# Tokens kept by residue modulo 4 in each tile of 128, and mixer D's bias table laid out whole

## The chip, the cores and the metric

The kernel runs on one core of a Trainium2 chip. The metric is the device time of one execution in microseconds (us); smaller is better.

## What is computed

Two layers of an encoder trunk over 512 tokens of 1024 features, all in float32. Each layer is a norm, one combined projection to the queries, keys and values of four attention mixers (A, B, C, D) and to four gate blocks, the mixers, their gated sum, an output projection, and an MLP:

```
h = rms_norm(x, attn_norm_g)
q, k, v of A, B, C, D and four gates = split(h @ w_in)
a = mixer_window_gqa(...)       # |i-j| <= 128
b = mixer_dilated(...)          # head groups: |i-j| <= 64 with step 1, <= 256 with step 4, <= 1024 with step 16
c = mixer_differential(...)     # dense, two softmaxes subtracted
d = mixer_neighbourhood(...)    # tokens as 8 rows x 64 columns, 16 columns seen, learned relative bias
x = x + (sum of sigmoid(gate) * (branch @ w_branch)) @ w_out
x = x + relu(rms_norm(x, mlp_norm_g) @ w_up)^2 @ w_down
```

In the second and third head group of B a query sees only tokens of its own residue modulo 4 (modulo 16).

## The kernel before

The 512 tokens are four tiles of 128. The normed input lies transposed in SBUF as two tiles `h_hi` and `h_lo` [128 features, 8, 512 tokens]: each float32 number is kept as a short-mantissa part (fp32r) and the rest of it. A product of two such operands is three matmuls on TensorE (PE), `mm3`, lines 285 to 287: hi by hi, hi by lo, lo by hi. With tokens on the output's partitions (`tm_steps`) the stationary operand is a block of `h`, 128 features by 128 tokens, and the weights stream past it; with features on the partitions (`fm_steps`) the weights are stationary. Each matmul has a weight load of its own ("PEld" in the profile), which may run beside the matmul before it.

Weights come as [128, 768] or [128, 512] units (`unit`): a DMA on the SyncE queue (SP) into `w_raw`, a rounding on ScalarE (ACT) into `w_hi`, a subtraction on VectorE (DVE) into `w_lo`. The first five units' subtraction runs on GpSimd (POOL), line 252.

`project` makes the queries, keys and values of a pair of heads for the token tiles t = 0 to 3. Lines 517 and 524 are those that the first part of the change is about:

```
toks = slice(t, S, NT) if order == "perm" else slice(t * P, (t + 1) * P)
...
if plain:
    nc.scalar.copy(vt[:, t, 0:4:3, :], pv)
```

Mixer B has `order == "perm"`: its token tile t is made of the tokens t, t+4, t+8 and so on, so the stationary block is taken from `h` with a step of four elements of 4 bytes. B has three such chunks in a layer, each with 4 token tiles, 8 feature tiles and 3 matmuls: 288 in a layer, 576 in all. All other blocks of `h` are taken with step one. `qk_norm` and `halves` then norm, rotate and split the heads, and `turn_heads` transposes them on PE and writes them to a `stack` tile [128, 2, 512] with `evacuate` on ACT (line 563). In the order "col" of mixer D that write puts token r * 64 + c at column c * 8 + r, so it has a step of 8 elements (32 bytes). B's order is "perm" and is written straight, 512 elements at a time. `turn_values` (line 572) reorders D's values in the same way, and `store` writes the outputs of B and D back to the tokens' order with a step in what it writes.

`plain` chunks are the second and third head group of B. Their values are copied from PSUM by one ACT instruction for a token tile.

Mixer D's mask tile `d_full` is the mask less the relative bias. The bias comes by 16 DMAs for each head (lines 774 to 776), each to 8 partitions; 128 in all, issued on SP, which also issues the weights' DMAs in its program order.

The order in which the chunks are projected is the list `STREAM`. A planner (`Plan`) interleaves these projections with the heads' attention by an estimate of what it has given to each engine, and the tile framework then sorts the instructions of each engine once more by a simulated time line. So a change of an instruction's shape can move others.

Of the kernel before, what the change touches and what calls it, by code (L numbers as in the profile page):

```python
# [10 lines left out]
F32 = mybir.dt.float32  # L11
# [8 lines left out]
P = 128  # L20
# [48 lines left out]
# Slots of the attention's tiles.  # L69
# [11 lines left out]
class Job:  # L81
    """A column chunk of the projections; left counts what is still to be put in place."""
# [80 lines left out]
class Net:  # L163
# [16 lines left out]
    def setup(self):  # L180
# [6 lines left out]
        self.rope64p = c.tile([P, 2, NT, 32], F32, name="rope64p")  # L187
        self.rope32n = c.tile([P, 2, NT, 16], F32, name="rope32n")
        nc.sync.dma_start(self.rope64n, I["rope64n"])
        nc.sync.dma_start(self.rope64p, I["rope64p"])  # L190
# [34 lines left out]
    def rsqrt(self, pool, ss, n, scale, tag, eng=None):  # L225
        """1 / sqrt(ss * scale + EPS) for a [128, n] tile."""
# [15 lines left out]
    def unit(self, layer, name, k0, kk, segs):  # L242
# [6 lines left out]
        if len(self.W.units) <= NPOOL:  # L249
            # The other engines are still at the first norm.  # L250
# [31 lines left out]
    def mm3(self, ps, st, mv, first, last):  # L282
        """ps += st.T @ mv for split operands (hi, lo); what both parts lack lies below float32."""
# [6 lines left out]
    def tm_steps(self, ps, act, toks, units):  # L290
        """Tokens on partitions: ps[128 tokens, n] = act[:, toks].T @ W."""
# [5 lines left out]
    def fm_steps(self, ps, act, units, c0, toks=slice(0, S)):  # L297
        """Features on partitions: ps[128 features, tokens] = W[:, c0:c0+128].T @ act."""
# [15 lines left out]
    def squares(self, pool, x, ms):  # L314
        """The sum of x^2 / D over the columns at hand."""
# [8 lines left out]
    def norm(self, pool, X, ms, g):  # L324
        """ms: for each token tile the parts of the mean square."""
# [77 lines left out]
    def flat_gain(self, pool):  # L403
        """The gains of mixer d, the queries' part times minus the scale."""
# [7 lines left out]
    def qk_norm(self, pool, ps, t, nq, nk, dh, rope=None, flat=None):  # L412
        """Norm and rotation of the nq + nk heads in ps[128 tokens, heads * dh]; [128, heads, dh]."""
# [61 lines left out]
    def project(self, pool, layer, job, order, segs, nq, nk, dh, rope=None, flat=None, plain=False, vcols=True):  # L475
        """One column chunk [q heads | k heads | v of a pair] for all tokens, transposed. job.q has
# [314 lines left out]
    def mixer_b(self, pool, layer):  # L791
        memo = {}

        def rope():
            if "r" not in memo:
                memo["r"] = self.rope_tables(pool, "b", self.rope64p)
# [422 lines left out]
```

## Time and profile before

| | |
|---|---|
| three executions | 1920.71, 1917.41, 1920.71 us (median 1920.71) |
| span of the profiled execution, first to last instruction | 1919.2 us |
| the profiled execution's own time | not told apart from the three; its span is 1.5 us below their median |
| busy: PE, weight loads, DVE, ACT, POOL | 1858.9, 1674.0, 1138.0, 852.6, 370.9 us |
| mean granted clock of TensorE | 0.990 of full speed |

Two attention stages, about 35 to 560 us and 985 to 1510 us, alternate with two MLPs. In the attention stages mixer D comes first, then A, B and C. [...] PE's busy time overlaps for neighbouring matmuls, so it is read best by the distance of their starts.

### The profile page before, as it was taken

The page shows a single profiled execution, that of the slowest core. Times are in us where ns is not written, and L with a number is a line of the kernel's source. Part 1 is how long each engine was busy: PE and PEld are TensorE (multiplying, and loading weights), DVE is VectorE, ACT ScalarE, POOL GpSimd, SP SyncE. Part 2 cuts the span into 40 slices and gives each one's busy share as a digit, 9 for nine tenths or more (in the row PEclk, how much of TensorE's full clock was granted, in tenths as well). Part 3 has the DMA queues.
Part 4 walks back from the last instruction along what each step waited for, and adds up shares of the span by engine and source line. Part 5 has one row for each costly group of instructions (what it writes and reads, how often), then busy time and mean ns, then how long its engine had stood idle before and what let it go on. Part 6 is the DMA issues. An engine that isn't in the chain of part 4 may idle for free.

```text
span 1919.2 us, 28303 instructions
## 1 busy us (share of the span) xinstructions
PE 1858.9 (97%) x10112; PEld 1674.0 (87%) x10112; DVE 1138.0 (59%) x2571; ACT 852.6 (44%) x1775; POOL 370.9 (19%) x1167
## 2 busy tenths in 40 slices
PE   6998999998999999999999899999999999999999
PEld 5997998886889899989989789988878898989899
DVE  6688756686665543443476876666876564443433
ACT  4666554555443432232357654545554344232321
POOL 3352353441200000000024604433512000000000
PEclk9999999998999999999999999999999999999999
DMA  4322122121242332333343211222222422233323
GB/s 155 102 81 75 50 70 76 50 79 57 77 147 87 105 96 88 88 96 98 122 131 90 86 50 42 76 70 61 68 64 81 146 86 93 88 102 99 94 88 107
DMA packets 70909, 168.96 MB, mean 88 GB/s; under 512 B 9456, under 2 KB 14704, under 8 KB 70768
## 3 DMA queue, kind: packets, MB, share of 16 engines
q1 hardware_dynamic: 70768, 167.16, 28.6%
q8 instruction: 79, 1.29, 0.3%
q14 instruction: 62, 0.51, 0.1%
HBM read 162.93 MB, written 4.19 MB: 87 GB/s over the span
## 4 chain that ended last, share of the span: by engine, by line
PE 82%; DVE 6%; POOL 4%; ACT 3%; issue 3%; DMA 2%; SPq 0%; POOLq 0%; DVEq 0%; ACTq 0%
PE mm L285 25%; PE mm L286 24%; PE mm L287 24%; PE tp L222 3%; PE s L594 2%; PE y L621 1%; POOL rs_w_qk L236 1%; PE y L620 1%; POOL rs_w_qk L235 1%; ACT stack L563 1%; DVE w_lo L216 1%; POOL rs_y_qk L238 1%; POOL rs_w_qk L237 1%; DMA w_raw<-in_wflat 1%; DMA x<-in_x 1%
## 5 line engine op out<-in xcount | busy, mean ns | idle before, releaser
L215 ACT CAST w_hi<-w_raw 128x768 fp32r<-128x768 f32 (+1 forms) x409 | 313.0, 772 | 430.9 <-PE mm L287 241.0
L216 DVE TENSOR_TENSOR w_lo<-w_raw,w_hi 128x768 fp32r<-128x768 f32 (+1 forms) x409 | 362.7, 892 | 191.0 <-ACT w_hi L215 164.9
L285 PE MATMUL mm<-h_hi,w_hi 128*128 128x512 f32 (+1 forms) x1104 | 425.9, 388 | 0.9 <-ACT h_hi L215 0.7
L286 PE MATMUL mm<-h_lo,w_hi 128*128 128x512 f32 (+1 forms) x1104 | 422.5, 384 | 1.4 <-DVE h_lo L216 1.4
L287 PE MATMUL mm<-h_hi,w_lo 128*128 128x512 f32 (+1 forms) x1104 | 416.8, 385 | 1.2 <-POOL w_lo L252 1.2
L287 PEld LDWEIGHTS mm<-h_hi,w_lo 128*128 128x128 f32 x1104 | 209.2, 190 | 41.5 <-POOL w_lo L252 1.7
L285 PEld LDWEIGHTS mm<-h_hi,w_hi 128*128 128x128 f32 x1104 | 209.0, 190 | 40.8 <-ACT h_hi L215 1.2
L286 PEld LDWEIGHTS mm<-h_lo,w_hi 128*128 128x128 f32 x1104 | 209.7, 190 | 39.5 <-DVE h_lo L216 1.8
L287 PE MATMUL mm<-w_hi,u_lo 128*128 128x384 f32 (+1 forms) x768 | 241.9, 319 | 0.0
L286 PE MATMUL mm<-w_lo,u_hi 128*128 128x384 f32 (+1 forms) x768 | 241.2, 319 | 0.0
L285 PE MATMUL mm<-w_hi,u_hi 128*128 128x384 f32 (+1 forms) x768 | 236.4, 319 | 0.0
L235 POOL TENSOR_TENSOR rs_w_qk<-rs_y_qk 128x4 f32<-128x4 f32 (+2 forms) x216 | 56.3, 261 | 782.5 <-DMA d_bias<-in_rel 455.9
L285 PE MATMUL mm<-w_hi,h_hi 128*128 128x384 f32 (+1 forms) x576 | 201.3, 355 | 3.3 <-ACT w_hi L215 1.4
L286 PE MATMUL mm<-w_lo,h_hi 128*128 128x384 f32 (+1 forms) x576 | 201.8, 352 | 0.3 <-DVE w_lo L216 0.2
L287 PE MATMUL mm<-w_hi,h_lo 128*128 128x384 f32 (+1 forms) x576 | 200.7, 350 | 0.0
L1081 DVE TENSOR_TENSOR x<-x,mm 128x384 f32<-128x384 f32 (+1 forms) x120 | 60.9, 508 | 186.9 <-PE mm L287 179.3
L287 PEld LDWEIGHTS mm<-w_hi,u_lo 128*128 128x128 f32 x768 | 143.7, 188 | 0.0
L285 PEld LDWEIGHTS mm<-w_hi,u_hi 128*128 128x128 f32 x768 | 143.1, 188 | 0.5
L286 PEld LDWEIGHTS mm<-w_lo,u_hi 128*128 128x128 f32 x768 | 143.2, 188 | 0.0
L285 PEld LDWEIGHTS mm<-w_hi,h_hi 128*128 128x128 f32 x576 | 135.4, 237 | 5.6 <-ACT w_hi L215 1.6
L286 PEld LDWEIGHTS mm<-w_lo,h_hi 128*128 128x128 f32 x576 | 136.4, 237 | 2.2 <-DVE w_lo L216 0.8
L287 PEld LDWEIGHTS mm<-w_hi,h_lo 128*128 128x128 f32 x576 | 136.4, 237 | 0.7
(166 smaller groups left out, 2916.7 us busy)
## 6 DMA issues: line engine op xcount, KB each, us to landing
w_raw<-in_wflat SPq DMA_DIRECT2D x296, 384.0 KB
w_raw<-in_wflat SPq DMA_DIRECT2D x112, 256.0 KB
x<-in_x SPq DMA_DIRECT2D x8, 512.0 KB
d_full<-in_mask_d SPq DMA_DIRECT2D x8, 448.0 KB
d_bias<-in_rel SPq DMA_DIRECT2D x128, 12.0 KB
x_save<-x SPq DMA_DIRECT2D x4, 512.0 KB
x<-x_save SPq DMA_DIRECT2D x4, 512.0 KB
out_y<-x SPq DMA_DIRECT2D x8, 192.0 KB
```

What stands on the lines that cost most here:

```text
L215: self.nc.scalar.copy(hi, src)
L216: self.nc.vector.tensor_tensor(lo, src, hi.bitcast(F32), op=ALU.subtract)
L222: self.nc.tensor.transpose(out, in_, self.ident_r if short else self.ident)
L235: eng.tensor_tensor(w, y, y, op=ALU.mult)
L236: eng.tensor_tensor(w, w, v, op=ALU.mult)
L237: eng.tensor_scalar(w, w, -0.5, 1.5, op0=ALU.mult, op1=ALU.add)
L238: eng.tensor_tensor(y, y, w, op=ALU.mult)
L285: nc.tensor.matmul(ps, st[0], mv[0], start=first, stop=False)
L286: nc.tensor.matmul(ps, st[0], mv[1], start=False, stop=False)
L287: nc.tensor.matmul(ps, st[1], mv[0], start=False, stop=last)
L594: self.nc.tensor.matmul(ps, q[:, qc], k[:, kc], start=i == 0, stop=i == len(ks) - 1)
L1081: nc.vector.tensor_tensor(x, x, ps[:, 0:w], op=ALU.add)
```

## The change

The tokens are put in another order on the host before the kernel and back after it. Within each tile of 128, place 32 * a + m holds token 4 * m + a: all tokens of one residue modulo 4 lie together. Then:

- B's projections take token tiles of step one, as the others do. The sorting into residue classes moves to `turn_heads`: two writes of 256 elements in runs of 32, in place of one write of 512. B's rotary table `rope64p` and its DMA go.
- The values of a plain chunk are put into their residue class by four ACT copies of 32 partitions, in place of one of 128.
- The first head group's scores read the keys in runs of 32 elements, and the mask in four blocks.
- D's reordering (stacks, values, the store) has runs of 4 elements (16 bytes) where it had single elements. A block of 128 places still holds 16 columns of all 8 rows. B's store has runs of 32.
- D's bias table is laid out on the host for all 128 query places, and comes by one DMA for each head: 8 in all in place of 128.
- The masks are made for the new order. Their sizes stay.

```
-            toks = slice(t, S, NT) if order == "perm" else slice(t * P, (t + 1) * P)
+            toks = slice(t * P, (t + 1) * P)
...
                 if plain:
-                    nc.scalar.copy(vt[:, t, 0:4:3, :], pv)
+                    for c in range(NT):
+                        nc.scalar.copy(vt[32 * t:32 * t + 32, c, 0:4:3, :], pv[32 * c:32 * c + 32])
...
             if order == "col":
-                r0 = (t // 2) * 4
+                g0 = (t // 2) * 16
                 for j in range(2):
-                    dst = st[:, j, :].rearrange("p (c r) -> p r c", r=8)[:, r0:r0 + 4, :]
-                    self.evacuate(dst, src[:, j].rearrange("p u (r c) -> p (u r) c", c=64))
+                    dst = st[:, j, :].rearrange("p (b g e) -> p g b e", b=4, e=4)[:, g0:g0 + 16]
+                    self.evacuate(dst, src[:, j].rearrange("p u (g b e) -> p (u g) b e", b=4, e=4))
+            elif order == "perm":
+                a0 = t - 1
+                for j in range(2):
+                    dst = st[:, j, :].rearrange("p (c a m) -> p a c m", c=NT, m=32)[:, a0:a0 + 2]
+                    self.evacuate(dst, src[:, j].rearrange("p u (c m) -> p u c m", m=32))
...
-        self.nc.scalar.copy(v_t.rearrange("p (c r) -> p r c", r=8), ps.rearrange("p (r c) -> p r c", c=64))
+        self.nc.scalar.copy(v_t.rearrange("p (b g e) -> p g b e", b=4, e=4), ps.rearrange("p (g b e) -> p g b e", b=4, e=4))
...
-                        for q in range(16):
-                            nc.sync.dma_start(bias[q * 8:q * 8 + 8, :],
-                                              I["rel"][layer, 2 * p + h, :, (15 - q) * 8:(15 - q) * 8 + 384])
+                        nc.sync.dma_start(bias[:, 0:384], I["rel"][layer, 2 * p + h])
...
-                self.scores(sp, jobs[0].q[i], jobs[0].k[i], cs, slice(0, S))
+                own = [k.rearrange("p (c a m) -> p a c m", c=NT, m=32) for k in jobs[0].k[i]]
+                for n, k in enumerate(own):
+                    nc.tensor.matmul(sp, jobs[0].q[i][:, cs], k, start=n == 0, stop=n == len(own) - 1)
...
-        self.store(pool, 1, y.rearrange("p (c j) -> p c j", c=NT), lambda x: x.rearrange("p (j c) -> p c j", c=NT))
+        self.store(pool, 1, y.rearrange("p (c a m) -> p c a m", c=NT, m=32),
+                   lambda x: x.rearrange("p (a c m) -> p c a m", c=NT, m=32))
...
+PLACE = np.arange(S)
+TOKEN = PLACE // P * P + 4 * (PLACE % 32) + PLACE % P // 32
...
-    arrays = {"x": a["x"].reshape(S, D), "rel": relative(a["d_rel_bias"]), **{k: a[k] for k in SMALL}, **constants()}
+    arrays = {"x": np.ascontiguousarray(a["x"].reshape(S, D)[TOKEN]), "rel": relative(a["d_rel_bias"]), **{k: a[k] for k in SMALL}, **constants()}
```

The framework sorts the instructions of the changed program anew, and many places of the attention stages differ by a few rows. The first place is POOL in layer 0, at D's first projection; `w_lo<-w_raw,w_hi` is the rest of a weight unit that PE waits for, and the `rs_` rows are the inverse square roots of `qk_norm`. Before, then in the changed program:

```order
L237 TENSOR_SCALAR rs_w_qk<-rs_w_qk 128x4
L238 TENSOR_TENSOR rs_y_qk<-rs_y_qk,rs_w_qk 128x4
L235 TENSOR_TENSOR rs_w_qk<-rs_y_qk 128x4
L236 TENSOR_TENSOR rs_w_qk<-rs_w_qk,rs_v_qk 128x4
L237 TENSOR_SCALAR rs_w_qk<-rs_w_qk 128x4
L238 TENSOR_TENSOR rs_y_qk<-rs_y_qk,rs_w_qk 128x4
L235 TENSOR_TENSOR rs_w_qk<-rs_y_qk 128x4
L252 TENSOR_TENSOR w_lo<-w_raw,w_hi 128x768
L236 TENSOR_TENSOR rs_w_qk<-rs_w_qk,rs_v_qk 128x4
```

```order
L235 TENSOR_SCALAR rs_w_qk<-rs_w_qk 128x4
L236 TENSOR_TENSOR rs_y_qk<-rs_y_qk,rs_w_qk 128x4
L250 TENSOR_TENSOR w_lo<-w_raw,w_hi 128x768
L233 TENSOR_TENSOR rs_w_qk<-rs_y_qk 128x4
L234 TENSOR_TENSOR rs_w_qk<-rs_w_qk,rs_v_qk 128x4
L235 TENSOR_SCALAR rs_w_qk<-rs_w_qk 128x4
```

The weight unit's row stands five rows earlier on POOL. The second place is ACT in layer 0, at the first plain chunk of B (`qk_n<-mm` and `v<-mm` empty a PSUM tile of the projection, `y_rest<-y` and `pt_hi<-tp` belong to A's heads):

```order
L419 COPY qk_n<-mm 128x256
L527 COPY v<-mm 128x2x64
L421 ACTIVATE qk_sq<-qk_n 128x256
L419 COPY qk_n<-mm 128x256
L527 COPY v<-mm 128x2x64
L639 COPY y_rest<-y 64x512
```

```order
L417 COPY qk_n<-mm 128x256
L527 COPY v<-mm 32x2x64
L646 COPY y_rest<-y 64x512
L527 COPY v<-mm 32x2x64 x3
L419 ACTIVATE qk_sq<-qk_n 128x256
L417 COPY qk_n<-mm 128x256
L527 COPY v<-mm 32x2x64 x4
```

A PSUM tile is free after four copies where it was free after one, and another copy can stand between them. The third place is SP in layer 0, where D's mask and bias are issued among the weights:

```order
L771 DMA d_full<-in_mask_d 128x896
L775 DMA d_bias<-in_rel 8x384 x15
L248 DMA w_raw<-in_wflat 128x768
L775 DMA d_bias<-in_rel 8x384
L771 DMA d_full<-in_mask_d 128x896
L775 DMA d_bias<-in_rel 8x384 x16
L248 DMA w_raw<-in_wflat 128x768 x7
```

```order
L778 DMA d_full<-in_mask_d 128x896
L781 DMA d_bias<-in_rel 128x384
L778 DMA d_full<-in_mask_d 128x896
L781 DMA d_bias<-in_rel 128x384
L246 DMA w_raw<-in_wflat 128x768 x8
```

Thirty issues less stand ahead of the weights there, and as many less at the second pair of D.

## Rows read from the trace of the kernel before

**Rows 1.** The page's busy times by engine: busy us (share of the span) xinstructions.

```profile
PE 1858.9 (97%) x10112; PEld 1674.0 (87%) x10112; DVE 1138.0 (59%) x2571; ACT 852.6 (44%) x1775; POOL 370.9 (19%) x1167
PE 82%; DVE 6%; POOL 4%; ACT 3%; issue 3%; DMA 2%; SPq 0%; POOLq 0%; DVEq 0%; ACTq 0%
```

**Rows 2.** Busy times by stretch: length, PE, PEld, DVE, ACT, POOL; clock, DMA, GB/s.

```profile
200.00:283.00 83.00, 83.00 (x417) 82.58 (x417) 53.27 (x158) 42.36 (x112) 38.55 (x139) 1.00 0.16 51
1150.00:1240.00 90.00, 87.87 (x440) 86.81 (x440) 59.12 (x172) 45.83 (x123) 37.92 (x141) 1.00 0.17 51
...
150.00:200.00 50.00, 45.51 (x227) 38.02 (x225) 40.43 (x100) 29.20 (x70) 5.17 (x12) 0.97 0.25 76
340.00:440.00 100.00, 99.39 (x534) 86.14 (x533) 78.50 (x193) 56.59 (x129) 42.01 (x125) 1.00 0.22 66
1050.00:1110.00 60.00, 50.54 (x282) 45.51 (x280) 48.72 (x138) 38.24 (x92) 33.25 (x105) 0.89 0.25 72
1300.00:1400.00 100.00, 98.96 (x527) 84.64 (x527) 77.32 (x180) 57.72 (x130) 41.10 (x118) 1.00 0.25 75
```

**Rows 3.** Weight loads by shape (busy, mean ns): B's stretch 195 to 285, then whole span.

```profile
L285 PEld LDWEIGHTS mm<-w_hi,h_hi 128*128 128x128 f32 x96 | 31.0, 326 | 0.1
...
L285 PEld LDWEIGHTS mm<-w_hi,u_hi 128*128 128x128 f32 x768 | 143.1, 188 | 0.5
```

**Rows 4.** Time line of PE, start and length in us: mixer B, then mixer D.

```profile
228.55 0.39 PE L285 MATMUL mm<-w_hi,h_hi 128*128 128x384 f32 x1
231.35 0.39 PE L285 MATMUL mm<-w_hi,h_hi 128*128 128x384 f32 x1
...
104.24 0.33 PE L285 MATMUL mm<-w_hi,h_hi 128*128 128x384 f32 x1
107.36 0.33 PE L285 MATMUL mm<-w_hi,h_hi 128*128 128x384 f32 x1
```

**Rows 5.** ACT groups by shape: count, busy us, mean ns, idle before.

```profile
L527 ACT COPY v<-mm 128x128 f32<-128x128 f32 x16 | 4.6, 286 | 0.0
L563 ACT CAST stack<-tp 128x512 fp32r<-128x512 f32 x36 | 20.0, 590 | 7.5 <-PE tp L222 7.2
L215 ACT CAST pt_hi<-tp 128x256 fp32r<-128x256 f32 x48 | 17.8, 372 | 36.9 <-PE tp L222 24.7 <-PE y L621 12.0
L563 ACT CAST stack<-tp 128x256 fp32r<-128x256 f32 x48 | 26.0, 729 | 0.0
```

**Rows 6.** The split of the branch outputs: shortest, median and longest ns.

```profile
L215 ACT CAST y_hi<-y_sum x18: 618/636/1133, 98.3 to 1482.6; 128x512 fp32r<-128x512 f32 x18
L216 DVE TENSOR_TENSOR y_lo<-y_sum,y_hi x18: 676/684/1127, 99.5 to 1483.3; 128x512 fp32r<-128x512 f32 x18
```

**Rows 7.** What PE waited for: us in total, times, longest.

```profile
PE mm L285 <- ACT y_hi L215: 4.8, 2, 4.2
PE tp L222 <- ACT stack L563: 0.7, 1, 0.7
PE mm L285 <- ACT v L527: 1.1, 1, 1.1
PE mm L286 <- DVE w_lo L216: 0.2, 1, 0.2
```

**Rows 8.** Time lines and chain at POOL's late weight unit: start, length, what.

```profile
41.23 0.83 ACT L251 CAST w_hi<-w_raw 128x768 fp32r<-128x768 f32 x1
...
42.72 1.78 POOL w_lo L252
...
44.54 0.50 PE L287 MATMUL mm<-h_hi,w_lo 128*128 128x512 f32 x1 [1.24 <-POOL w_lo L252]
```

**Rows 9.** SP's queue: D's bias issues by length, a run of them, its longest wait.

```profile
L775 SPq DMA_DIRECT2D d_bias<-in_rel x128: 271/293/376, 33.2 to 1045.0; - x128
...
1033.03 12.30 SPq L775 DMA_DIRECT2D d_bias<-in_rel  x32
...
SPq L248 <- DVE w_lo L216: 1177.4, 321, 21.9
```

**Rows 10.** A slow-clock stretch of layer 1: the window, and two chain pieces in it.

```profile
1100.00:1105.00 5.00, 1.32 (x3) 1.09 (x4) 4.14 (x13) 3.57 (x8) 2.34 (x6) 0.50 0.02 5
...
1104.90 0.43 PE mm L286
1105.33 0.43 PE mm L287
```

More of the change, by code (lines that the diff above doesn't have):

```diff
@@ L186, in setup @@
         self.rope64n = c.tile([P, 2, NT, 32], F32, name="rope64n")
-        self.rope64p = c.tile([P, 2, NT, 32], F32, name="rope64p")
         self.rope32n = c.tile([P, 2, NT, 16], F32, name="rope32n")
         nc.sync.dma_start(self.rope64n, I["rope64n"])
-        nc.sync.dma_start(self.rope64p, I["rope64p"])
         nc.sync.dma_start(self.rope32n, I["rope32n"])
@@ L715, in local_head @@
             else:
-                self.store(pool, m, pair.y.rearrange("p (c r) -> p c r", r=8), back)
+                self.store(pool, m, pair.y.rearrange("p (b g e) -> p b g e", b=4, e=4), back)
             plan.give("prob")
@@ L783, in mask_of @@
                 return lambda b, k0: f[:, half, 384:640] if b == 0 else f[:, half, 640:896] if b == NT - 1 else f[:, half, 0:384]
-            back = lambda x: x.rearrange("p (r c) -> p c r", c=64)
+            back = lambda x: x.rearrange("p (g b e) -> p b g e", b=4, e=4)
             for i in range(2):
@@ L795, in rope @@
             if "r" not in memo:
-                memo["r"] = self.rope_tables(pool, "b", self.rope64p)
+                memo["r"] = self.rope_tables(pool, "b", self.rope64n)
             return memo["r"]
@@ L827, in dilated @@
                 sp = self.sps.tile([P, S], F32, name="s", tag="s")
-                self.scores(sp, jobs[0].q[i], jobs[0].k[i], cs, slice(0, S))
+                own = [k.rearrange("p (c a m) -> p a c m", c=NT, m=32) for k in jobs[0].k[i]]
+                for n, k in enumerate(own):
+                    nc.tensor.matmul(sp, jobs[0].q[i][:, cs], k, start=n == 0, stop=n == len(own) - 1)
+                    self.pe(S)
                 yield 0.05
@@ L837, in dilated @@
                 pn = thin[c // 2][:, c % 2, :]
-                nc.vector.tensor_tensor_reduce(pw, sp, mask[:, (3 - c) * P:(7 - c) * P], scale=1.0, scalar=TOP,
+                tiles = lambda x: x.rearrange("p (a x) -> p a x", a=NT)
+                nc.vector.tensor_tensor_reduce(tiles(pw), tiles(sp), tiles(mask[:, 0:896])[:, :, 32 * (3 - c):32 * (7 - c)],
+                                               scale=1.0, scalar=TOP,
                                                op0=ALU.add, op1=ALU.min, accum_out=m0[:, 0:1])
@@ L1156, in run @@
                     self.hT = self.norm(pool, X, ms, g)
+PLACE = np.arange(S)
+TOKEN = PLACE // P * P + 4 * (PLACE % 32) + PLACE % P // 32
+GRID = np.stack([TOKEN[16 * (np.arange(P) // 4) + 4 * b + np.arange(P) % 4] for b in range(NT)])
+GRID_ROW, GRID_COL = GRID // 64, GRID % 64
 def constants():
@@ L1164, in rope @@
         return np.ascontiguousarray(np.stack([np.cos(ang), np.sin(ang)], axis=1).astype(np.float32))
-    p, t = np.arange(P)[:, None], np.arange(NT)[None, :]
-    c = {"rope64n": rope(t * P + p, 64), "rope64p": rope(t + NT * p, 64), "rope32n": rope(t * P + p, 32)}
+    own = TOKEN.reshape(NT, P).T
+    c = {"rope64n": rope(own, 64), "rope32n": rope(own, 32)}
     far = lambda bad: np.where(bad, np.float32(BIG), np.float32(0)).astype(np.float32)
-    i = np.arange(P)[:, None]
-    c["mask_a"] = far(np.abs(np.arange(384)[None, :] - P - i) > 128)
-    x = np.arange(896)[None, :]
-    c["mask_b"] = far(np.abs(4 * (x % P - i) + (x // P - 3)) > 64)
-    j = np.arange(P)[None, :]
+    c["mask_a"] = far(np.abs(TOKEN[None, 0:384] - TOKEN[P:2 * P, None]) > 128)
+    i, j, x = np.arange(P)[:, None], np.arange(P)[None, :], np.arange(896)[None, :]
+    c["mask_b"] = far(np.abs(4 * (x // 224 * 32 + x % 32 - i) + (x % 224 // 32 - 3)) > 64)
     c["mask_b2"] = np.concatenate([far(np.abs(i - j) > 64), far((i - j) % 4 != 0)], axis=1)
-    qc = np.arange(P)[:, None] // 8
     parts = []
-    for b, k0, n in ((1, 0, 384), (0, 128, 256), (3, 0, 256)):
-        q = 16 * b + qc
-        k = 16 * (b - 1) + (k0 + np.arange(n)[None, :]) // 8
+    for b, k0, n in ((1, 0, 3), (0, 0, 2), (3, 2, 2)):
+        q = GRID_COL[b][:, None]
+        k = GRID_COL[k0:k0 + n].reshape(1, -1)
         c0 = np.clip(q - 8, 0, 48)
@@ L1189, in relative @@
     n, h = bias.shape[:2]
-    out = np.zeros((n, h, 8, 63, 8), bias.dtype)
-    for qr in range(8):
-        out[:, :, qr, 16:47, :] = bias[:, :, 7 - qr:15 - qr, :].transpose(0, 1, 3, 2)
-    return out.reshape(n, h, 8, 63 * 8)
+    dr = GRID_ROW[0:3].reshape(1, -1) - GRID_ROW[1][:, None] + 7
+    dc = GRID_COL[0:3].reshape(1, -1) - GRID_COL[1][:, None] + 15
+    wide = np.concatenate([bias.reshape(n, h, -1), np.zeros((n, h, 1), bias.dtype)], axis=2)
+    return np.ascontiguousarray(wide[:, :, np.where((dc >= 0) & (dc < 31), dr * 31 + dc, 15 * 31)])
 SMALL = ["attn_norm_g", "a_qk_norm_g", "a_sink", "b_qk_norm_g", "c_qk_norm_g", "c_lambda", "c_subln_g",
@@ L1217 @@
     r = run_bass_kernel_spmd(nc, [{f"in_{k}": v for k, v in arrays.items()}], core_ids=[0])
-    return r.results[0]["out_y"].reshape(1, S, D)
+    y = r.results[0]["out_y"]
+    return y[np.argsort(TOKEN)].reshape(1, S, D)
```

## The prediction

> **What bounds the kernel now.** I read the page's busy times first. PE is busy for 97% of the span and holds 82% of the chain of waits; the next engine, DVE, is busy for 59% [rows 1]. So an edit counts by what it does to PE: by PE's own time, or by a wait that PE then has. Next I read the busy times by stretch, because the attention stages are not like the MLPs. B's projections lie at about 200 to 283 us and 1150 to 1240 us. PE is busy there for all but 2.1 us of 173, and the weight loads are as busy as the matmuls (82.58 and 86.81 us). In the other attention stretches PEld stands well below PE, as 86.14 against 99.39 [rows 2]. The reader is to see that in B's stretches, and only there, TensorE waits for its own weight loads.
>
> The groups by shape say why. A load of the same 128x128 block takes 326 ns where the tokens are taken with a step of four, and 188 ns with step one [rows 3]. On PE's time line the matmuls of 384 columns then start further apart. In B two starts of L285, with twelve matmuls from the first to the second, are 231.35 - 228.55 = 2.80 us apart: 0.2333 us each. In D, with step one, eighteen matmuls take 107.36 - 104.24 = 3.12 us: 0.1733 us each [rows 4]. Both stretches are at full clock and without a wait.
>
> **The change part by part.** The sum is made against the profiled execution's span, 1919.2 us. Its own time is not told apart; the span is 1.5 us below the median of the three runs, and I take 1.5 us as what lies around it. About 0.2% (3.8 us) is what a measurement here can tell from no change.
>
> *Weight loads with step one.* 576 matmuls (96 of each of the three lines in a layer) by 0.2333 - 0.1733 = 0.060 us: **-34.6 us**. All of it is PE's own time, and PE did not wait there. The bounds: the whole difference of the loads, 576 by 0.138 = 79 us, can't come, since the matmuls then set the pace as they do in D; the lower end is nothing (a rival below). I take the pitch, because it was measured for the same shape in both forms.
>
> *What covered other engines in B's stretches.* They shrink from 83 and 90 us to 65.7 and 72.7, with the same 53.3 and 59.1 us of DVE in them, mostly A's heads: DVE's share goes from 64 and 66% to 81%. Stretches with step one and 77 to 81% of DVE are in the trace: PE stood idle for 4.49 of 50 us, 0.61 of 100, 9.46 of 60 and 1.04 of 100 [rows 2], together 15.6 of 310, 5.0%. On 138.4 us that is 7.0 us; 2.1 are there now: **+4.8 us**. By the best of these rows it would be -1.3 us, by the worst +19.7. I take the mean, since the work is of the same kind and nothing tells which is nearest.
>
> *Four copies of values for one.* A copy of 128 elements takes 286 ns [rows 5]. 16 become 64, on 32 partitions each; the number of elements of a partition stays, so I take the same 286 ns: 13.7 us more of ACT, and 0.86 us more until a PSUM tile of a projection is free. ACT has 42.4 us of work in the 83 us stretch; with 6.9 us more in 65.7 it is at about 75%. PE waited once for such a copy, 1.1 us [rows 7]. I let two waits grow: **+1.7 us**. The ends are nothing and all 16 tiles, 13.8 us.
>
> *B's writes in two halves.* 20 writes of 512 at 590 ns become 40 of 256 in runs of 32 elements. The nearest row is a straight write of 256 from PSUM, 372 ns; the other end is D's write with single elements, 729 ns [rows 5]. 3.1 us to 17.4 us more of ACT, and I take the lower end, for a run of 32 is nearer to straight than to single. Its cover is PE's projections of the next tiles; PE waited for a stack for 0.7 us in the whole span [rows 7]. **0.**
>
> *D's writes in runs of four.* 48 writes at 729 ns go to somewhere between 372 and 729 ns: 0 to 17.1 us of ACT saved. I take 0.4 us for one, since three elements of four follow their neighbour. For the same reason as above it is **0** on the path, with 0.7 us at most directly.
>
> *The stores.* The split of an output takes 0.64 us on ACT and 0.68 us on DVE in the median, and 1.13 us each at its longest, which are the six pairs of B and D [rows 6]. PE waited twice for `y_hi`, 4.8 us in all [rows 7]. Two times 0.50 us for hi, and 0.4 us once for lo: **-1.4 us**. The ends are nothing and all six pairs, 5.6 us.
>
> *POOL's order.* The fifth weight unit's rest was computed from 42.72 us, behind `qk_norm`'s rows. Its `w_hi` was there at 41.23 + 0.83 = 42.06, and PE stood idle for 1.24 us until it was done [rows 8]. Five rows earlier, it waits for `w_hi` alone: **-0.7 us** (0 to -1.2).
>
> *D's bias in 8 DMAs.* 120 issues less by 0.293 us are 35 us of SP's queue, in runs as long as 12.3 us, with weights behind them [rows 9]. SP has room: it waited for 1177 us for DVE to free weight buffers, and PE waited for a DVE weight unit for 0.2 us in all [rows 7, 9]. So they are hidden behind loads that run ahead: **0**. If that cover were gone, one run of issues would hold a weight back by its 12.3 us; the change shortens that too.
>
> *The rest.* The first group's scores read the keys in runs of 32, 32 matmuls; between nothing and the stepped load's 0.060 us each, 1.9 us; I take nothing, for the same reason of nearness. The mask in four blocks leaves DVE's elements as they are. `rope64p`'s load is one DMA in the first microseconds. **0.** The order of the instructions is drawn anew throughout the attention stages; that has no sign, and I give it some 8 us either way in the range, half of the 15.6 us that PE stood idle in the four stretches above.
>
> The sum: -34.6 + 4.8 + 1.7 - 1.4 - 0.7 = -30.2; 1919.2 - 30.2 + 1.5 = **1890.5 us**.
>
> **The rivals.**
>
> *Cover lost.* B's stretches become like the worst of the four stretches, +19.7 instead of +4.8: 1905.4 us. For it: DVE at 81% there and long chains from scores to probabilities, and ACT gets 16.8 us more of work in the same stretches. Against it: two of the four stretches lost 1% or less. Chance 0.17.
>
> *D gains more than its stores.* PE was idle in the two stretches after D, 150 to 200 and 1050 to 1110 us, for 4.49 and 9.46 us, and the clock was 0.97 and 0.89 of full there, some 0.03 x 50 + 0.11 x 60 = 8.1 us more [rows 2]. With D's writes, values and stores shorter, two thirds of these 22 us may go: 1890.5 - 14.5 = 1876.0 us. Against it: the waits there are for DVE as well, which D's change relieves little. Chance 0.17.
>
> *Slower: B's stretches fall to the low clock.* [...] Chance 0.03.
>
> *No gain: the step is not what makes the loads long.* The starts in B would stay 0.233 us apart for another reason. Then the loads and the cover stay, and the small terms give 1920.7 + 1.7 - 1.4 - 0.7 = 1920.3 us. Against it stand the 326 and 188 ns for blocks of one size and type. Chance 0.02. [...]
>
> **How the numbers follow.** The forecast has 0.61, the rivals 0.17, 0.17, 0.03 and 0.02. The forecast and the first two are faster by over 0.2%: 0.95. The fourth is within 0.2%: 0.02. The third is slower: 0.03. The range reaches past the second rival to 1874 and to the first one's 1905.4, rounded to 1906. It leaves out the last two rivals, and the tails in which the new order or the copies' wait (13.8 us at most) add to the cover lost.
>
> **What would show it.** Right: PEld for L285 to L287 with 384 columns at 188 ns throughout, starts 0.173 us apart in B's stretches, B's stretches some 15 us shorter each; `v` copies 64 of about 0.29 us; D's stack writes at about 0.4 us; the y splits at about 0.65 us throughout; SP with 8 bias issues; PE's idle time up by a few us in B's stretches, the clock at 1.00 there. Wrong: the loads still above 300 ns; or the loads at 188 ns and PE idle for more than 10 us in a stretch of B, behind probabilities or behind `v`; or a clock of 0.50 in one. The MLPs, whose code is the same, should keep their times.

## The result, and the profile after

The changed kernel takes 1895.53 us (median of four runs, 1893.15 to 1896.65), beside 1919.06 us for the kernel before on the same chip: the ratio is 0.9879, interval 0.9865 to 0.9893. That is 23.5 us faster, where 30.2 was forecast; the time lies in the range, and on the side that was given 0.95.

The page's busy times and its chain of waits, of the kernel after (line numbers have moved: L285 to L287 are now L283 to L285):

```profile
PE 1829.3 (97%) x10112; PEld 1639.2 (87%) x10112; DVE 1137.9 (60%) x2571; ACT 851.2 (45%) x1843; POOL 377.0 (20%) x1167
PE 81%; DVE 7%; POOL 5%; issue 3%; ACT 2%; DMA 2%; SPq 0%; POOLq 0%; DVEq 0%; ACTq 0%
```

Against [rows 1] PE is busy for 29.6 us less, and the span, 1893.9 us, is 25.3 us shorter: PE's idle time went from 60.3 to 64.6 us. TensorE is still the bound.

The group of the projections' weight loads shows the first term:

```profile
L283 PEld LDWEIGHTS mm<-w_hi,h_hi 128*128 128x128 f32 x576 | 109.4, 191 | 2.9 <-ACT h_hi L213 0.8 <-ACT w_hi L213 0.7 <-ACT v L527 0.7
```

This group holds the loads of A, B, C and D in one; B's 326 ns [rows 3] are gone from its mean. PE's time line in B's stretch has the products as [rows 4] had them in D:

```profile
229.96 0.33 PE L283 MATMUL mm<-w_hi,h_hi 128*128 128x384 f32 x1
...
230.48 0.35 PE L283 MATMUL mm<-w_hi,h_hi 128*128 128x384 f32 x1
```

Three starts further on are 0.52 us, 0.173 us a matmul.

To see where the rest went I cut both spans at the first product of a stage in PE's time line: the first one of B's projections, and the first one that takes `m` (the end of the attention). In us:

| Stretch | before | after | difference |
|---|---|---|---|
| start to B, layer 0 | 197.70 | 205.50 | +7.8 |
| B to the end of attention, layer 0 | 358.56 | 345.45 | -13.1 |
| rest of layer 0, to A's projections of layer 1 | 473.47 | 471.31 | -2.2 |
| A's projections to B, layer 1 | 119.85 | 114.43 | -5.4 |
| B to the end of attention, layer 1 | 358.45 | 343.77 | -14.7 |
| rest of layer 1 | 411.17 | 413.44 | +2.3 |

B's part gave back 27.8 us. In front of it layer 1 won 5.4 us, and layer 0 lost 7.8. That loss is what the experiments had to find. Six matmuls more stand in front of B in layer 0 of the new order and four more in layer 1, about 1 us each time, so the cuts compare nearly the same work. The MLPs kept their times but for one piece: the last row's 2.3 us. At 1490 to 1500 us, right behind layer 1's attention, the clock is 0.83 in the kernel after. Two runs below that have its order show the long row too (413.8 us each); all other orders have 411.1 to 412.0 us. So this piece belongs to the order.

The windows of the kernel before, and then of the kernel after, in the same 20 us of it (length, PE, PEld, DVE, ACT, POOL; clock, DMA, GB/s):

```profile
40.00:60.00 20.00, 18.39 (x89) 14.23 (x88) 13.90 (x37) 10.80 (x23) 11.96 (x37) 1.00 0.38 116
```

```profile
40.00:60.00 20.00, 16.36 (x74) 12.95 (x73) 12.39 (x34) 6.92 (x18) 12.07 (x36) 0.91 0.36 123
```

15 matmuls fewer were done in it, and the clock was 0.91. A second hole is at 155 us, and layer 1 has one behind D's outputs; PE's time line and windows of the kernel after:

```profile
159.69 0.47 PE L220 MATMUL tp<-ident,prob 128*128 128x128 f32 x1 [4.95 <-DVE prob L699]
1091.19 1.29 PE L283 MATMUL mm<-y_hi,w_hi 128*128 128x512 f32 x2 [4.63 <-ACT y_hi L213]
```

```profile
155.00:160.00 5.00, 0.32 (x2) 0.32 (x3) 3.38 (x8) 4.39 (x11) 3.33 (x9) 0.50 0.31 100
1090.00:1095.00 5.00, 3.81 (x9) 2.92 (x10) 4.70 (x16) 2.11 (x4) 1.22 (x3) 0.50 0.25 80
```

The kernel before had holes at both places. In layer 0 its hole was the smaller one:

```profile
155.00:160.00 5.00, 4.67 (x16) 4.02 (x17) 5.00 (x12) 1.92 (x6) 1.56 (x3) 0.66 0.27 80
```

In layer 1 it was the larger one: PE was idle for 9.3 us from 1090 to 1105 us (a part of it is in [rows 10]), where it is now idle for 5.0 us from 1085 to 1095 us. The granted clock was 0.50 of full speed in the windows of the two waits above. Behind the second wait PE works slowly: the first two products take 1.29 us together and the next ones, of 512 columns, start 0.43 us apart, where such products start 0.23 us apart at 1080 to 1084 us, at a clock of 1.00. So a wait of 5 us costs somewhat more than 5.

### The profile page after: what moved, and what is told of

Read it like the earlier page. It is cut to its first block, busy times and chain, and to the rows that moved or that the text cites. A ratio compares the mean times of both kernels' runs of the same rounds, so it can differ in the third digit from the quotient of the medians.

```text
span 1893.9 us, 28237 instructions
## 1 busy us (share of the span) xinstructions
PE 1829.3 (97%) x10112; PEld 1639.2 (87%) x10112; DVE 1137.9 (60%) x2571; ACT 851.2 (45%) x1843; POOL 377.0 (20%) x1167
## 3 DMA queue, kind: packets, MB, share of 16 engines
q1 hardware_dynamic: 69728, 167.03, 28.2%
q8 instruction: 79, 1.29, 0.3%
## 4 chain that ended last, share of the span: by engine, by line
PE 81%; DVE 7%; POOL 5%; issue 3%; ACT 2%; DMA 2%; SPq 0%; POOLq 0%; DVEq 0%; ACTq 0%
PE mm L283 24%; PE mm L284 24%; PE mm L285 24%; PE tp L220 4%; PE s L601 2%; POOL rs_w_qk L233 1%; PE y L628 1%; PE y L627 1%; DVE w_lo L214 1%; POOL rs_w_qk L234 1%; POOL rs_y_qk L236 1%; POOL rs_w_qk L235 1%; DMA x<-in_x 1%; PE s L841 0%; PE y L886 0%
## 5 line engine op out<-in xcount | busy, mean ns | idle before, releaser
L283 PE MATMUL mm<-h_hi,w_hi 128*128 128x512 f32 (+1 forms) x1104 | 424.7, 387 | 1.8 <-DVE sig L1026 1.0
L285 PE MATMUL mm<-h_hi,w_lo 128*128 128x512 f32 (+1 forms) x1104 | 417.0, 385 | 4.3 <-POOL w_lo L250 2.3
L285 PEld LDWEIGHTS mm<-h_hi,w_lo 128*128 128x128 f32 x1104 | 209.1, 190 | 44.4 <-DVE w_lo L214 3.1
L283 PEld LDWEIGHTS mm<-h_hi,w_hi 128*128 128x128 f32 x1104 | 209.1, 190 | 43.0 <-DVE sig L1026 2.9
L285 PE MATMUL mm<-w_hi,u_lo 128*128 128x384 f32 (+1 forms) x768 | 241.9, 319 | 0.0
L283 PE MATMUL mm<-w_hi,u_hi 128*128 128x384 f32 (+1 forms) x768 | 236.4, 319 | 0.0
L233 POOL TENSOR_TENSOR rs_w_qk<-rs_y_qk 128x4 f32<-128x4 f32 (+2 forms) x216 | 62.3, 288 | 786.6 <-DMA subln<-in_c_subln_g 474.7
L285 PE MATMUL mm<-w_hi,h_lo 128*128 128x384 f32 (+1 forms) x576 | 189.3, 330 | 2.6 <-DVE h_lo L214 2.6
L284 PE MATMUL mm<-w_lo,h_hi 128*128 128x384 f32 (+1 forms) x576 | 189.5, 331 | 1.8 <-DVE w_lo L214 1.7
L283 PE MATMUL mm<-w_hi,h_hi 128*128 128x384 f32 (+1 forms) x576 | 188.1, 332 | 1.4 <-ACT w_hi L213 0.5
L285 PEld LDWEIGHTS mm<-w_hi,u_lo 128*128 128x128 f32 x768 | 143.7, 188 | 0.0
L283 PEld LDWEIGHTS mm<-w_hi,u_hi 128*128 128x128 f32 x768 | 143.1, 188 | 0.5
L284 PEld LDWEIGHTS mm<-w_lo,h_hi 128*128 128x128 f32 x576 | 109.9, 191 | 3.5 <-DVE w_lo L214 2.7
L285 PEld LDWEIGHTS mm<-w_hi,h_lo 128*128 128x128 f32 x576 | 109.9, 191 | 3.6 <-DVE h_lo L214 2.9
L283 PEld LDWEIGHTS mm<-w_hi,h_hi 128*128 128x128 f32 x576 | 109.4, 191 | 2.9 <-ACT h_hi L213 0.8
```

The lines of the kernel that those rows point to most:

```text
L233: eng.tensor_tensor(w, y, y, op=ALU.mult)
L283: nc.tensor.matmul(ps, st[0], mv[0], start=first, stop=False)
L284: nc.tensor.matmul(ps, st[0], mv[1], start=False, stop=False)
L285: nc.tensor.matmul(ps, st[1], mv[0], start=False, stop=last)
```

## The experiments

Two theories stood at the start. *Cover*: what is missing of the 30.2 us was lost in B's shorter stretches. *Order*: the change draws another order of instructions in the rest of the attention stages, and that costs.

**The step alone, in the old order.** B's projections of the kernel before take tokens in a row; the order on every engine stays.

```diff
-            toks = slice(t, S, NT) if order == "perm" else slice(t * P, (t + 1) * P)
+            toks = slice(t * P, (t + 1) * P)
```

> The kernel before with one edit: B's projections take token tiles of step one. (B's heads then see other tokens than they should; the work and the order of the instructions on every engine are the same as before.) Theory A, cover: the 34.6 us of the weight loads come, and about 10 us of them are given back in B's stretches, because DVE and ACT no longer keep up there; expects 1919 - 25 = 1894 us and PE idle in B's stretches, as in the changed kernel. Theory B, order: the loads give nearly all of their 34.6 us, and what is missing in the changed kernel comes from the new order of its instructions elsewhere; expects 1919 - 32 = 1887 us.

Measured: 1885.69 us, ratio 0.9820 (0.9806 to 0.9834), 33.2 us less than before. That is near *order*'s 1887 us.

**The step put back into the kernel after**, the same line the other way, and the order stays.

> The changed kernel with one edit: B's projections take their tokens with step four again. (B's heads then see other tokens than they should; the work and the order of the instructions are those of the changed kernel.) Theory A, cover: back to the kernel before, less the small gains of D's shorter writes: 1917 us. Theory B, order: slower than the kernel before, by what the new order costs: 1924 to 1928 us.

Measured: 1923.77 us, ratio 1.0024 (1.0016 to 1.0033). So the step is worth 28.2 us in the new order, and the rest of the change costs 4.9 us by itself: had B's tokens kept their step, the change would have been a loss. This too is near *order*'s figure.

The windows from B's first product to C's, both layers, with the sum behind them, say why 28 and not 33 us. First the kernel before and the one with the step taken out of it, then the kernel after with the step and the kernel after:

```profile
197.70:328.55 130.85, 130.85 (x640) 121.22 (x639) 86.07 (x244) 64.27 (x160) 58.94 (x196) 1.00 0.20 63
1149.58:1283.53 133.95, 131.82 (x644) 121.66 (x643) 88.18 (x250) 65.25 (x163) 56.72 (x196) 1.00 0.21 62
```

```profile
196.56:312.22 115.66, 113.38 (x640) 102.26 (x638) 85.10 (x244) 63.09 (x160) 59.72 (x196) 1.00 0.24 72
1132.08:1248.12 116.04, 113.71 (x645) 103.09 (x643) 87.73 (x250) 63.70 (x162) 58.60 (x196) 1.00 0.24 71
```

```profile
203.99:333.08 129.09, 129.09 (x623) 119.38 (x621) 81.91 (x238) 70.27 (x187) 59.22 (x196) 1.00 0.21 63
1148.63:1278.45 129.82, 129.82 (x627) 120.13 (x627) 83.54 (x239) 70.46 (x189) 58.58 (x196) 1.00 0.21 62
```

```profile
205.50:320.90 115.40, 111.93 (x623) 100.32 (x622) 81.49 (x238) 69.00 (x187) 60.05 (x196) 1.00 0.23 70
1136.70:1252.20 115.50, 112.00 (x628) 101.01 (x627) 84.08 (x239) 70.27 (x190) 59.27 (x196) 1.00 0.23 70
```

The reader is to see two columns, the length and PE. In the new order PE's busy time falls from 258.91 to 223.93 us, by 35.0, and its idle time rises from 0 to 230.90 - 223.93 = 7.0 us: 28.0 us net, as the runs say. In the old order busy falls by 262.67 - 227.09 = 35.6 and idle rises from 2.1 to 4.6 us: 33.1 net. With the step in it, B's stretch was so slow that PE hardly waited (0 and 2.1 us); without it, the other engines set a part of the pace. The clock was 1.00 in all eight windows.

**D's bias by one DMA, in the kernel before.** The table is laid out whole, and the order is drawn anew (1310 rows of PE differ from the kernel before).

```diff
-                        for q in range(16):
-                            nc.sync.dma_start(bias[q * 8:q * 8 + 8, :],
-                                              I["rel"][layer, 2 * p + h, :, (15 - q) * 8:(15 - q) * 8 + 384])
+                        nc.sync.dma_start(bias[:, 0:384], I["rel"][layer, 2 * p + h])
```

> The kernel before with D's bias by one DMA for each head and nothing else; its instructions are sorted anew. Theory A, cover: 1919 us within 3. Theory B, order: 1922 to 1927 us.

Measured: 1929.28 us, ratio 1.0047 (1.0034 to 1.006): 10.4 us slower by the medians, 9.0 by the ratio, and more than either theory had.

**D's bias by 16 DMAs again, in the kernel after** (the order is drawn anew here too).

> The changed kernel with D's bias fetched by 16 DMAs for each head again, from the table laid out whole. This changes 120 DMA issues and, through the framework's sorting, the order of the instructions. Theory A, cover: the bias is hidden either way, 1895 us within 3. Theory B, order: the order that came with the single DMA is what costs; 1887 to 1891 us.

Measured: 1894.60 us, ratio 0.9865 (0.985 to 0.988): within a microsecond of the kernel after, which is *cover*'s figure. Taken by the total, the two runs contradict each other: one bias DMA costs 10.4 us in one kernel and about 1 in the other. By stretches they agree on one place. From the start to B's first product in layer 0, with 16 DMAs a head: 197.70 (before), 196.56 (the step alone) and 199.20 us (this run). With one: 208.43 (the run above), 203.99 (after with the step) and 205.50 us (after). No other part of the change goes with that split: the kernel before with one DMA has none of them, and this run has all. So in front of B the order that comes with one DMA is 6.3 us slower in the kernel after and 10.7 in the kernel before. This run loses 3.6 us of its 6.3 again further on: from B to the end of attention it takes 344.28 and 347.54 us, 2.6 us more than the kernel after in the two layers, and 1.0 us more from A to B in layer 1. (The execution that was profiled is the fastest of its four; its span is 4.1 us below that of the kernel after, where the medians are 0.9 us apart.)

These microseconds are not lost at one place. Up to the first product of D's second projection, 252 matmuls from the start in each of the six kernels, those with 16 DMAs take 63.0 (before), 62.2 (the step alone) and 64.0 us (this run), those with one 64.8, 65.5 and 66.2 us: 2.2 us are lost by then in the kernel after, 1.8 in the kernel before. The windows from there to B's first product, first of the kernel after and of this run, then of the kernel before and the run above:

```profile
66.20:205.50 139.30, 129.66 (x761) 116.25 (x760) 107.48 (x303) 87.30 (x226) 52.00 (x169) 0.96 0.25 81
64.00:199.20 135.20, 129.18 (x762) 117.35 (x761) 105.95 (x302) 86.30 (x223) 50.90 (x169) 0.96 0.28 83
```

```profile
63.00:197.70 134.70, 127.63 (x755) 114.79 (x754) 106.64 (x298) 89.88 (x219) 50.44 (x169) 0.99 0.27 83
64.80:208.40 143.60, 132.06 (x761) 117.90 (x760) 108.78 (x301) 90.73 (x223) 52.64 (x169) 0.94 0.25 78
```

Another 4.1 and 8.9 us are lost here. PE's largest waits in it are the one for `prob` at 159.69 us in the kernel after, shown above, and in the run above this one:

```profile
PE mm L285 <- ACT y_hi L215: 5.0, 1, 5.0
```

The longest single wait in the same stretch is 1.3 us in the kernel before and 2.8 us in this run. Both long waits end at 159 us, over 100 us behind the bias, where D's last outputs and A's first probabilities come due together. Which rows of the new orders make them is not shown.

What happens in the first part, at 40 us, is in DVE's time line, first of the kernel before, then of the kernel after:

```profile
42.82 3.35 DVE L216 TENSOR_TENSOR w_lo<-w_raw,w_hi 128x768 fp32r<-128x768 f32 x2 [1.01 <-ACT w_hi L215]
...
48.61 1.22 DVE L778 TENSOR_TENSOR d_full<-d_full,d_bias 128x384 f32<-128x384 f32 x3
```

```profile
42.21 2.85 DVE L783 TENSOR_TENSOR d_full<-d_full,d_bias 128x384 f32<-128x384 f32 x3
...
45.64 1.22 DVE L783 TENSOR_TENSOR d_full<-d_full,d_bias 128x384 f32<-128x384 f32 x3
...
47.26 1.82 DVE L214 TENSOR_TENSOR w_lo<-w_raw,w_hi 128x768 fp32r<-128x768 f32 x2
```

With one DMA the subtraction of the bias stands ahead of the weights' rests in DVE's queue. It runs from 42.21 us and takes 2.85 instead of 1.22 us; the rests, at 42.82 us before, come at 47.26. The 2.85 us are no wait for the bias: its row names none, and one of its three subtractions alone is long, 2.02 us where the same shape takes 0.42:

```profile
43.04 2.02 DVE L783 TENSOR_TENSOR d_full<-d_full,d_bias 128x256 f32<-128x256 f32 x1
```

Beside it POOL worked on a weight unit, from 42.80 to 44.78 us (its row is shown in the next section). DVE waits for a landing of the bias only in layer 1, twice; the last line is from the view of the DMA issues (issue to landing last, us):

```profile
978.55 0.90 DVE L783 TENSOR_TENSOR d_full<-d_full,d_bias 128x384 f32<-128x384 f32 x2 [1.35 <-DMA d_bias<-in_rel]
...
1030.10 2.37 DVE L783 TENSOR_TENSOR d_full<-d_full,d_bias 128x384 f32<-128x384 f32 x6 [2.76 <-DMA d_bias<-in_rel]
```

```profile
d_bias<-in_rel SPq DMA_DIRECT2D x8, 192.0 KB, 4.7
```

No loss is seen there: from D's first product to B's in layer 1 the kernel after takes 175.8 us, this run 177.6.

PE has a hole behind 42 us in both. In the kernel after it waits for POOL's unit, and its products of 512 columns then start 0.43 us apart, at a clock of 0.50 from 45 to 47 us; in this run, with 16 DMAs, it waits for rows of the norm:

```profile
44.83 0.80 PE L285 MATMUL mm<-h_hi,w_lo 128*128 128x512 f32 x1 [2.25 <-POOL w_lo L250]
45.42 0.63 PE L283 MATMUL mm<-h_hi,w_hi 128*128 128x512 f32 x1
45.85 0.63 PE L284 MATMUL mm<-h_lo,w_hi 128*128 128x512 f32 x1
```

```profile
45.04 0.28 PE L220 MATMUL tp<-ident_r,qk_s 128*128 128x128 f32 x1 [2.69 <-DVE qk_s L468]
```

The clock of 0.91 is not what loses the 15 matmuls. The run with the step put back has the order of the kernel after, a clock of 1.00 in the same window, and 73 matmuls in it:

```profile
40.00:60.00 20.00, 15.09 (x73) 11.68 (x72) 12.16 (x32) 6.91 (x20) 12.03 (x36) 1.00 0.32 107
```

In one kernel the early subtraction is seen to hold PE, the kernel before with one DMA: rows that PE waits for come on DVE right behind it.

```profile
43.48 1.22 DVE L776 TENSOR_TENSOR d_full<-d_full,d_bias 128x384 f32<-128x384 f32 x3
44.61 0.61 DVE L470 TENSOR_TENSOR qk_s<-qk_n,qk_s 128x128 fp32r<-128x128 f32 x2
44.95 0.45 PE L222 MATMUL tp<-ident_r,qk_s 128*128 128x128 f32 x3 [3.18 <-DVE qk_s L470]
```

So about 2 us of the 6.3 and 10.7 go with the subtraction's earlier place on DVE, none of them with a wait for its landing, and the rest comes with the new order further on.

**D's writes in single elements**, as before, in the kernel after; the order on every engine stays.

```diff
-                    dst = st[:, j, :].rearrange("p (b g e) -> p g b e", b=4, e=4)[:, g0:g0 + 16]
-                    self.evacuate(dst, src[:, j].rearrange("p u (g b e) -> p (u g) b e", b=4, e=4))
+                    dst = st[:, j, :].rearrange("p (c r) -> p r c", r=8)[:, g0 // 4:g0 // 4 + 4, :]
+                    self.evacuate(dst, src[:, j].rearrange("p u (r c) -> p (u r) c", c=64))
...
```

The values' copy and the two lines of the store go back in the same way.

> The changed kernel with D's stacks, values and stores written in single elements with a step of 8, as before. (D's tokens are then not where its masks look for them; the work and the order of the instructions on every engine stay.) Theory B, order, with D's shorter writes as what made up for part of it: 1897 to 1901 us, that is 2 to 6 us slower than the changed kernel. Rival: D's writes were hidden, as the prediction had most of them; 1895 to 1896.5 us.

Measured: 1903.99 us, ratio 0.9916 (0.99 to 0.9931), beside 0.9879: D's shorter writes are worth 8.5 us by the medians, 7.1 by the ratios. ACT's groups by shape, first with single elements, then in the kernel after:

```profile
L570 ACT CAST stack<-tp 128x256 fp32r<-128x256 f32 x72 | 33.8, 608 | 1.8 <-PE tp L220 1.5
L213 ACT CAST y_hi<-y_sum 128x512 fp32r<-128x512 f32 x18 | 13.2, 731 | 9.7 <-DVE y_sum L991 7.6 <-DVE y_sum L647 2.0
L579 ACT COPY v_t<-mm 128x512 f32<-128x512 f32 x4 | 4.7, 1185 | 0.7 <-PE mm L285 0.7
```

```profile
L570 ACT CAST stack<-tp 128x256 fp32r<-128x256 f32 x72 | 22.2, 395 | 2.8 <-PE tp L220 2.5
L213 ACT CAST y_hi<-y_sum 128x512 fp32r<-128x512 f32 x18 | 11.2, 621 | 10.1 <-DVE y_sum L991 8.0 <-DVE y_sum L647 2.0
L579 ACT COPY v_t<-mm 128x512 f32<-128x512 f32 x4 | 2.4, 596 | 0.7 <-PE mm L285 0.7
```

48 of the 72 stack writes are D's: (608 - 395) x 72 / 48 = 320 ns less for each, so 409 from 729 [rows 5]. ACT's busy time goes from 865.3 to 851.2 us. So about half of these 14.1 us were on the path. The execution that was profiled is the slowest of its five, with a span 12.8 us longer than that of the kernel after. In it the time from A to B in layer 1 is 118.06 us, against 114.43, and from the start to B in layer 0 208.40, against 205.50.

**One copy of B's values** for four, in the kernel after (125 rows of PE differ).

```diff
-                    for c in range(NT):
-                        nc.scalar.copy(vt[32 * t:32 * t + 32, c, 0:4:3, :], pv[32 * c:32 * c + 32])
+                    nc.scalar.copy(vt[:, t, 0:4:3, :], pv)
```

> The changed kernel with one copy of the values of a plain chunk for a token tile, as before. (The values then lie in another order than the probabilities; 48 copies less on ACT. The framework moves 125 of PE's rows.) Theory B, order: 1895 us within 3. Rival: the five microseconds that the loads give less in the new kernel are the copies' doing, by PSUM tiles that come free later; 1890 us or less.

Measured: 1893.45 us, ratio 0.9857 (0.984 to 0.9874), 2 us below the kernel after, with intervals that overlap.

**Another order with the same work.** The planner's delay `CHAIN` is 9; in the kernel after it is set to 8, and then to 10.

> The changed kernel with CHAIN = 8.0 in place of 9.0: the planner lets a head's transposes go on 1 us earlier. Same work, another order of the instructions. Theory B, order: the order alone moves the time by several us, so this may lie anywhere from 1884 to 1906 us. Rival, the order is worth little: 1895.5 us within 2.

> The changed kernel with CHAIN = 10.0: the same the other way. Theory B, order: from 1884 to 1906 us, not the time of the run with 8.0. Rival: 1895.5 us within 2.

Measured: 1916.51 us (ratio 0.9982, 0.9973 to 0.9991) and 1920.34 us (1.0000, 0.9991 to 1.0009). With every instruction the same, two other orders give back 21 and 25 us by the medians (20 and 23 by the ratios), nearly all and all that the change had brought. PE's waits with 10:

```profile
PE mm L283 <- ACT y_hi L213: 14.5, 2, 7.5
PE tp L220 <- DVE c_rb L985: 9.4, 2, 4.7
```

For 9 these are 4.6 and 5.0 us. About half of both losses lies at one place: from C's first projection to the end of the attention the two layers take 9.0 us more with 8, and 11.6 with 10, of spans that are 19.4 and 24.8 us longer. What a delay of 8 or 10 does to the kernel before was not run.

**One delay alone.** Of the two uses of the delay, the one ahead of mixer C's last turn of `c_rb` is made 13 instead of 9: in the kernel before, in the kernel after, and in the kernel after with 16 bias DMAs.

```diff
-        yield CHAIN
+        yield CHAIN + 4.0
```

> The kernel before with one number changed: the delay ahead of mixer C's last turn of c_rb is 13 instead of 9, so the order of some instructions is drawn anew while the work and all DMAs stay (338 rows of PE differ, against 1310 in the kernel before with one bias DMA). Theory 'order alone costs': a redraw with no change of the work moves the time by some us either way, within 10 us of 1919, and the extra 10.4 us of the single bias DMA need no cost of the DMA itself. Rival 'the bias DMA itself costs': a redraw without it stays within 2 us of 1919.

> The kernel after with the same one number changed (257 rows of PE differ). PE waited for c_rb for 5.0 us in the kernel after; if that wait is what is gained, 1895.5 - 3 to 5 = about 1891; theory 'order alone moves': anywhere within 10 us of 1895.5.

> The kernel after with D's bias by 16 DMAs a head again and the longer delay ahead of c_rb. With 16 DMAs alone it was 1894.6; if the longer delay is worth 3 to 5 us there, about 1890.5; if it is worth nothing, 1894.6.

Measured: 1930.87 us (ratio 1.0061, 1.0046 to 1.0077), 1906.62 us (0.9934, 0.9919 to 0.9949) and 1903.82 us (0.9921, 0.9906 to 0.9936): 11.0, 11.1 and 9.2 us slower than their own kernels. For the last two my expectation was wrong in its sign: PE's wait for `c_rb` did not shrink, it grew. PE's waits with the longer delay in the kernel before:

```profile
PE tp L222 <- DVE c_rb L973: 9.3, 2, 4.7
PE mm L285 <- ACT sig L996: 7.2, 6, 2.2
PE s L967 <- ACT c_y L962: 4.1, 2, 2.1
```

The wait for `c_rb` was 5.0 us in the kernel before. From B to the end of attention the layers take 363.24 and 364.38 us instead of 358.56 and 358.45, so 10.6 us lie there (of 13.5 in the profiled execution, the slowest of its four). As I read the waits, C's last turn is among the last work of that stage, and what is delayed there has nothing behind it to fill PE. That is also why this is no fair trial of *order* in general: it is a loss at one known place, of like size in three kernels, and not a random draw. The first of the three lies a microsecond beyond what *order alone* allowed, and far from its rival's 2 us.

**B's first chunk earlier.** In the kernel after, B's first column chunk goes ahead of D's second branch chunk (584 rows of PE differ).

```diff
-STREAM = "D0 gD1 D1 A0 A1 gD2 zD2 gD0 zD0 zD1 B0 B1 B2 ...
+STREAM = "D0 gD1 D1 A0 A1 gD2 zD2 gD0 zD0 B0 zD1 B1 B2 ...
```

> The kernel after with B's first column chunk ahead of D's second branch chunk in the stream (584 rows of PE differ, same work). D's branch products then stand further from the split of D's outputs and the next ones get cover: if PE's waits in 150 to 165 us and 1085 to 1095 us are what is lost there, some 5 us less, 1890; theory 'order alone moves': anywhere within 10 us of 1895.5, and no better than that.

Measured: 1893.30 us, ratio 0.9866 (0.9849 to 0.9882). It is 2.2 us below the kernel after, by intervals that overlap; the wait for `y_hi` stays at 4.6 us. No other order of this work was found that is shown to beat the kernel after.

## Why the prediction was right, and where its terms were off

*Weight loads, -34.6 us*: right. PE's busy time in B's stretches fell by 35.0 us in one order and 35.6 in the other. The rival by which the step does not matter is out: with step one the starts in B are 0.173 us apart, not 0.233.

*Cover lost, +4.8 us*: right in kind and near in size. PE's idle time there rose by 7.0 us in the new order, and by 2.5 in the old one.

*Four copies, +1.7 us*: not contradicted; the run with one copy is 2 us faster, within the intervals. The copies took 256 ns, not the 286 of [rows 5], and PE waited for `v` for 0.5 us, less than the 1.1 of [rows 7]. So the 2 us, if they are real, are not a wait for `v`; ACT's time or the 125 rows that moved are left.

```profile
L527 ACT COPY v<-mm 32x128 f32<-32x128 f32 x64 | 16.4, 256 | 0.9
```

*B's writes in two halves, 0*: no run has them alone. 16 of the 40 can be read by themselves, at 373 ns, so the lower end that was taken for a write was right.

*D's writes in runs of four, 0, "0.7 us at most directly", and the stores, -1.4 us*: this step was mis-sized. The duration was right (0.4 us taken, 0.41 measured; the splits took 620 and 686 ns at the median and 639 and 852 at the longest, against 1133 and 1127 [rows 6]). The path was not: together they are worth 7 to 8.5 us. I had read PE's waits for a stack, 0.7 us [rows 7], as the whole of what ACT's writes cost. My reading, which no run parts further, is that a long write also holds back the halves, splits and gates behind it on ACT, and that these carry other names in the list of waits: with single elements PE's idle time is 4.7 us longer, 2.0 of it in waits for `pt_lo`, and its busy time 8.1 us at a lower clock (0.983 against 0.986). The rival by which D gains more had the direction, and in layer 1 the place: A to B is 5.4 us shorter there. In layer 0 it had not: PE was still idle for 8.3 us of the 55.5 between 150 us and B. (A slip stands in this rival's sum: two thirds of 22 us are 14.7, not 14.5.)

*POOL's order, -0.7 us*: wrong. PE's wait there grew from 1.24 [rows 8] to 2.25 us. `w_hi` was there at 40.27 + 0.82 = 41.09, earlier than before, but rows of the norm still stood ahead on POOL, and the unit began at 42.80. There were five of them fewer, but they began at 39.37 us instead of 36.59: they take values from DVE, and DVE had waited for two small loads, 1.49 us for `gain_d` and 1.71 us for `sink`, waits that the kernel before does not have there.

```profile
40.27 0.82 ACT L249 CAST w_hi<-w_raw 128x768 fp32r<-128x768 f32 x1
```

```profile
42.46 0.38 POOL L236 TENSOR_TENSOR rs_y_qk<-rs_y_qk,rs_w_qk 128x4 f32<-128x4 f32 x1
42.80 1.98 POOL L250 TENSOR_TENSOR w_lo<-w_raw,w_hi 128x768 fp32r<-128x768 f32 x1
```

*D's bias by 8 DMAs, 0, "hidden behind loads that run ahead"*: the landing is hidden, as far as PE shows, but the term was not worked out to its end. I costed SP's queue and stopped there. The fewer issues change where the subtraction comes in DVE's order, and in layer 0 it then stands ahead of the weights' rests. Some 2 us are lost by D's second projection. With the rest of the order that comes with it, the loss from the start to B is 6.3 us in one kernel and 10.7 in the other; in total it is 9 to 10.4 in the kernel before, and not to be seen in the kernel after.

*The order, "no sign, some 8 us either way"*: too narrow. Two other orders of the same work are 21 and 25 us slower, none found is more than some 2 us faster, and a delay of 4 us at one place costs 9 to 11.

The sum with the measured terms: -35.0 + 7.0 + 2 - 8.5 = -34.5, against -23.5. The 11.0 us between are what the new order costs. In size they are near the 10.4 of the bias DMA in the kernel before, but they are not the DMA's alone: the run with 16 DMAs gives back 0.9 of them. 2.2 us of them are seen at the start of layer 0 and 2.3 behind layer 1's attention; the rest is left open. So the large term, the loads, was right for the reason that was given. That the total came out within 7 us of the forecast is in part luck: D's writes gave some 6 to 7 us that the sum did not have, against 11 us that the order took.

## What to carry to other kernels

When TensorE is the bound and its weight loads are as busy as its matmuls, look at the step of the stationary operand: laying the data out so that this step is one took the cost away (B's loads of 326 ns [rows 3] took 188 from 205.5 to 285 us of the kernel after), and of TensorE's own time it gave the full computed price; 28 to 33 of the 35 us were left once the other engines set a part of the pace. Price an edit on DMAs not by its queue alone but by what the new order puts ahead of the engine that feeds TensorE: list what the consumer of that DMA now stands in front of. When a row is long, look whether it waited or ran slowly beside another engine before you name the wait. And a planner's constants are part of the kernel: here the same instructions in another order gave back all of the gain.

## What the runs showed of the hardware

- A step of 16 bytes in the stationary operand made a load 326 ns instead of 188 [rows 3], and 576 matmuls 35.0 to 35.6 us longer. Why a load with the step takes longer is not shown.
- ACT's writes into SBUF show a like cost: 256 elements took 729 ns in single elements [rows 5], 409 in runs of four and 372 straight; 512 took 1185 and 596 ns.
- A copy of 32 partitions by 128 elements took 256 ns, one of 128 partitions by 128 elements 286 ns [rows 5]: a quarter of the partitions saved a tenth of the time.
- One DMA of 192 KB over 128 partitions took 4.7 us from issue to landing in the median.
- Beside the rest of a weight unit on POOL some DVE rows that read two tiles of SBUF took long. In the kernel after a subtraction of the bias began at 43.04 us, while POOL worked on such a unit (42.80 to 44.78 us), and took 2.02 us, where the same shape takes 0.42 elsewhere. In the kernel before a weight's rest on DVE began at 42.82 us, beside POOL's unit of 42.66 to 44.48 us, and took 2.48 us, where the next one takes 0.94. In the kernel after with 16 DMAs a row of the norm took 1.96 us from 42.05 us, where another takes 0.43; whether POOL had such a unit then is not shown here. A split that reads PSUM and SBUF, 0.68 us, kept its time beside such units (16.96 us in the kernel after, with three units on POOL from 13.01 to 18.78 us).
